# A third scan stage prepared inside the last convolution of a bidirectional RWKV-7 step

## The chip, the core and the metric

The kernel runs on one core of one Trainium2 chip. The metric is the device time of one execution in microseconds (us). The core's engines are PE (TensorE, matrix products; PEld is its weight load), DVE (VectorE), ACT (ScalarE), POOL (GpSimd) and SP (SyncE, which here only issues DMAs). Each engine executes its own instructions in a fixed order, and an instruction that waits holds up the ones behind it on that engine. SBUF is the on-chip memory of 128 partitions, PSUM the small memory in which PE leaves its results.

## The reference, cut to what matters

One layer of a diffusion backbone over 2176 tokens (128 of context, 2048 latent) and 1024 channels: a modulated RMS norm, one input projection, two head groups, one output projection.

```python
h = _rmsnorm(x, norm_g) * (1 + scale) + shift
r, k, v, g_a, b_gate, c_gate, u_conv, g_b = split(h @ w_in)
ya, s_final = _wkv(h, r, k, v, s0)                 # group A: 8 heads of 64, two directions
yb = b_gate * _short_conv(c_gate * u_conv, conv_w) * silu(g_b)      # group B
u = concat([ya * silu(g_a), yb]) @ w_out
out = x + gate * u

# inside _wkv, per token, head and direction:
s_kk = S @ kk_t
S = S * w_t - s_kk (kk_t * a_t)^T + v_t k_t^T
y_t = S @ r_t
```

The state S is a 64 by 64 matrix per head and direction. The kernel does not go token by token: it takes chunks of 64 tokens, for which the recurrence becomes matrix products with the inverse of a triangular matrix.

## The kernel before, in words

**Phase 1** (`phase1`) works on tokens in six blocks, two blocks to a third (`THIRD`). Each third has a recurrence part (`recurrence`: dense products for r, k, v and gate, and the operands of the scan, which go to DRAM as `scr_ops`, 1 MB per stage and direction when read back) and then a convolution part: `groupB` for four channel groups g and the third's two blocks j, eight units in all. Each unit has four dense products (`mmc`, `mmu`, `mmgb`, `mmb`) of 24 matmuls, three per 128 input channels (lines 182 to 184), since each float32 operand is split in a high and a low part. Weight blocks are read by `load_w`: in the first third raw (`raw_w`, tag `wr`, two buffers of 4 KB per partition, in pool `p1w`) and split; the split form is kept in DRAM (`scr_wsp`) and read from there in the later thirds (tag `w`, four buffers). `gate_rows`, run in the second third, uses the `wr` buffers too.

**Phase 2** (`phase2`) is the scan. 17 stages (`stages`), each of 8 chunks per direction gi = 0, 1, go through a software pipeline:

- `L` loads the operands into `rr` (one tile per direction, no second buffer);
- the first products `Gm`, `Fm` (line 1019, 32 small matmuls a direction) and `Qm` (line 1028, 4 transposes a direction) go through PSUM to the slot tiles F, GA and Q by `Ge`, `Fe` (DVE, line 1037), `Fa`, `Qe` (ACT). There are three slots (`B.slots`), and stage s has slot s modulo 3;
- `dg`, `ab` (DVE, line 1063), `zi` (ACT, lines 1072 to 1075), `pre` (DVE, lines 1081 and 1082) prepare, and `I` (`inverse`, POOL, lines 1091 and 1094, 45 instructions) makes the inverses of 32 by 32 blocks in the tile `zt`, of which there are two buffers;
- `zr`, `zd` (DVE, lines 1102 and 1105) transpose it, `U`, `bu`, `W`, `n` (PE line 1119, ACT 1122, PE 1127, ACT 1130; `c0`, `c1` on ACT, line 1111) merge pairs of blocks, `X`, `Xc` (PE 1171, ACT 1175) and `E`, `Ev` (PE 1189, DVE 1194) make the chunk operators, and `gh` copies GA and Q (ACT, lines 1160 and 1161) next to their operands;
- `S`, `sv`, `y` carry the state through the chunks (PE 1220, DVE 1246, ACT 1267).

`SEQ` is one body of the pipeline: `Gm1+3` in body b stands for stage b + 3. Bodies -3 to -1 are a prologue; from body 0 on PE, DVE and ACT have their order written out by hand (`manual_schedule`), and the last bodies follow `LATE`. POOL and SP there, and everything in the convolution and the prologue, are ordered by a planner from its own estimates, earlier lines of the program first.

**The seam between the phases.** In the last third's convolution the generator `early` runs beside the units, four steps after each unit. It opens phase 2's first pools on the right side of SBUF (`setup_first`) and emits the products and inverses of the first stages by `first(s)`, six steps a stage. `main` then opens the rest (`setup_rest`), on the left side where phase 1's pools were, and emits the prologue, which skips what is done already (`done`). A pool's memory can be used again when the tiles that lay there are released; slot 2 was in the pool `p2r2` of `setup_rest`.

Of the kernel before, what the change touches and what calls it, by code (L numbers as in the profile page):

```python
# [62 lines left out]
def phase1(K):  # L63
# [3 lines left out]
    wp = Pool(K, "p1w", "left", 2)  # L67
    hl = Pool(K, "p1h", "left", 2)
    tp = Pool(K, "p1t", "left")
    ca = Pool(K, "p1ca", "right")  # L70
    hr = Pool(K, "p1hr", "right")
    ta_ = Pool(K, "p1ta", "right")
# [68 lines left out]
        return w  # L141

    def raw_w(cb):
        raw = wp.tile([128, 8, 128], F32, tag="wr", name=f"wr{cb}_{K.u()}", bufs=2)
        nc.sync.dma_start(raw[:], A["win"][cb])
        return raw

# [475 lines left out]
    def gate_rows():  # L623
        for b in range(2):
            pr = None
            for k2 in range(4):
                wt = wp.tile([128, 2, 512], F32, tag="wr", name=f"wgate{b}{k2}", bufs=2)
                nc.sync.dma_start(wt[:], A["wada"][4 + b][:, k2 * 2:k2 * 2 + 2])
                yield
                pr = pr or pax.tile([128, 512], F32, tag="ax", name=f"psgr{b}")  # L630
                mod_rows(pr, wt, (k2 * 2, k2 * 2 + 1))
            rows = tp.tile([128, 512], F32, tag="pv", name=f"gaterow{b}", bufs=1)
            P.copy(rows[:], pr[:])
            yield
            pg = pax.tile([2, 512], F32, tag="ax", name=f"psgate{b}")
            T.matmul(pg[:], sel[:], rows[:], start=True, stop=True)
            gr = tp.tile([2, 512], F32, tag="pv", name=f"gate{b}", bufs=1)
            nc.sync.dma_start(gr[:], A["bgate"][:, b * 512:(b + 1) * 512].broadcast_to((2, 512)))
            V.tensor_tensor(gr[:], pg[:], gr[:], ALU.add)
            nc.sync.dma_start(S["gate"][:, b * 512:(b + 1) * 512], gr[:])  # L640
# [32 lines left out]
    for t3, js in enumerate(THIRD):  # L673
        wd, wi = wlora if t3 == 0 else (load_w(32), load_w(33))
        lws = {}
        pre = {}
        for j in js:
            if j not in hs:
                if t3 == 0:
                    pre[0] = psf[2:]  # L680
                    ws = ws0 + [load_w(cb) for cb in (8, 12)]
                    nc.sync.dma_start(smask[:], A["cst"][:, 128:512])
                run(make_h(j, xb[j]))
            lws[j] = lora_down(j, wd, wi, psf[:2] if j == 0 else None)
        if t3 == 0:
            load_up()
        if t3:
            ws = [load_w(cb) for cb in (4, 0, 8, 12)]
        wts = dict(zip("krvg", ws))
        following = {}  # L690
        recurrence(t3, [(g, j) for g in range(4) for j in js], js, lws, pre.pop(0, None), following)
        early = iter(()) if t3 != 1 else (x for f in (first_states, gate_rows) for x in f())
        if t3 == 2:
            for p in (pax, ta_, hr, ca):
                p.close()
            early = K.early()
        for g in range(4):
            ws = [load_w(cb + g) for cb in (20, 24, 28, 16)] if g else [wts[x] for x in "krvg"]
            for j in js:
                groupB(g, j, ws, hs[j], following)  # L700
                following = {}
                for _ in range(4 if t3 == 2 else 2):
                    next(early, None)
            if g == 1 and t3 < 2:
                j, j2 = THIRD[t3 + 1]
                run(make_h(j, norm(j, load_x(j))))
                xb[j2] = norm(j2, load_x(j2))
        for _ in early:
            pass
# [106 lines left out]
def phase2(K):  # L816
# [8 lines left out]
    def setup_first():  # L825

        O.r0 = Pool(K, "p2r0", "right")
        O.rI = Pool(K, "p2rI", "right")
        O.r1 = Pool(K, "p2r1", "right")
        O.pm = Pool(K, "p2m", "right", 2, PSUM)  # L830
        B.msk = O.r0.tile([128, 4, 128], F32, name="msk")
        B.mkg = O.r0.tile([128, 2, 128], F32, name="mkg")
        for i, j in enumerate((0, 2, 4, 5)):
            D(B.msk[:, i], A["msk"][:, j, 0:128])
        for i, j in enumerate((1, 3)):
            D(B.mkg[:, i], A["msk"][:, j, 64:192])
        B.I2 = O.r0.tile([128, 64], F32, name="I2")
        D(B.I2[:], A["i2"])
        B.idt = O.r0.tile([128, 128], F32, name="idt2")
        D(B.idt[:], A["idt"])  # L840
        B.hm = O.r0.tile([128, 2], F32, name="hm")
        D(B.hm[:], A["cst"][:, 514:516])
        B.ph = O.r0.tile([128, 3], F32, name="ph")
        D(B.ph[:], A["cst"][:, 516:519])
        B.slots = []
        for i in range(2):
            new_slot(O.r0)
        B.rr = ring(O.r1, 2, [128, 5, 8, 64], "rr", presetR)

    def new_slot(pool):  # L850
        i = len(B.slots)
# [9 lines left out]
    def setup_rest():  # L861
        O.l0 = Pool(K, "p2l0", "left")
        O.l1 = Pool(K, "p2l1", "left")
        O.pS = Pool(K, "p2S", "left", 4, PSUM)
        O.p2 = Pool(K, "p2s", "left", 2, PSUM)
        O.r2 = Pool(K, "p2r2", "right")
        new_slot(O.r2)
        cp = O.l0
        vec = cp.tile([128, 4], F32, name="vec2")
        D(vec[:], A["vec"][:, V_GW:V_GW + 4])  # L870
        B.gwh = cp.tile([128, 4], F32, name="gwh")
        V.tensor_scalar(B.gwh[:], vec[:], 0.5, None, ALU.mult)
        B.geps = cp.tile([128, 1], F32, name="geps")
        V.memset(B.geps[:], 64e-5)
        B.pc = cp.tile([64, 2, 8, 34], F32, name="pc")
        for d in range(2):
            D(B.pc[:, d], S[f"pc{d}"].rearrange("(e c) n -> c e n", c=64))

        B.fs = ring(O.l1, 2, [128, 2, 2, 8, 64], "stf", presetS)
        B.gs = ring(O.l1, 2, [128, 2, 2, 8, 64], "stg", presetS)  # L880
        B.gs2 = ring(O.r2, 2, [128, 2, 2, 8, 64], "sth", presetS)
        B.zb = O.l1.tile([128, 16, 64], F32, name="zb")
        zero(B.zb)
# [489 lines left out]

    def early():
        setup_first()
        for s in range(2):
            yield from first(s)

    seq = [(w.split("+")[0], int(w.split("+")[1]) if "+" in w else 0) for w in SEQ.split()]
# [6 lines left out]
    def main():  # L1386
# [10 lines left out]
        for word in LATE.split():  # L1397
            n, t = word.split("@")
            if n == "R":
                O.pm.close()  # L1400
                O.r2.close()
                O.r1.close()
                K.last["R"]()
                K.body = NST
            elif n == "Lo":
                for p in (O.p2, O.l1):
                    p.close()
                K.last["Lo"]()
            elif "." in t:
                next(ends[tuple(int(c) for c in t.split("."))], None)  # L1410
            elif n in K.last:
                K.last[n](int(t))
            else:
                do(n, int(t))
# [234 lines left out]
```

## Time and profile before

| | us |
|---|---|
| median of 3 runs | 1580.28 (1579.95 to 1585.35) |
| profiled execution, first to last instruction | 1578.3 |
| its device time around the span | not listed; 2.0 against the median |
| PE busy | 1499.9 (95%) |
| DVE, ACT, POOL busy | 1139.9, 772.3, 573.8 |
| mean granted TensorE clock | 0.982 |

The span is one execution seen by the hardware profiler. Phase 1 takes the first 947 us, the scan's bodies go to about 1340 us with the output projection beginning in between, and the rest is the output projection. In the rows of the profile a number with us is a time from the span's start; psGm, psFm, psQm are the PSUM tiles of Gm, Fm and Qm, `mm...` those of dense products. A busy time of POOL leaves out the short gap between two of its instructions.

### The profile page before, as it was taken

The page shows a single profiled execution, that of the slowest core. Times are in us where ns is not written, and L with a number is a line of the kernel's source. Part 1 is how long each engine was busy: PE and PEld are TensorE (multiplying, and loading weights), DVE is VectorE, ACT ScalarE, POOL GpSimd, SP SyncE. Part 2 cuts the span into 40 slices and gives each one's busy share as a digit, 9 for nine tenths or more (in the row PEclk, how much of TensorE's full clock was granted, in tenths as well). Part 3 has the DMA queues.
Part 4 walks back from the last instruction along what each step waited for, and adds up shares of the span by engine and source line. Part 5 has one row for each costly group of instructions (what it writes and reads, how often), then busy time and mean ns, then how long its engine had stood idle before and what let it go on. Part 6 is the DMA issues. An engine that isn't in the chain of part 4 may idle for free.

```text
span 1578.3 us, 39371 instructions
## 1 busy us (share of the span) xinstructions
PE 1499.9 (95%) x16208; PEld 1381.2 (88%) x16208; DVE 1139.9 (72%) x1957; ACT 772.3 (49%) x1462; POOL 573.8 (36%) x962
## 2 busy tenths in 40 slices
PE   5999999999999999999999998999999998899998
PEld 2899999999999999899998997888888886678786
DVE  5999995764999735449985428798998997746533
ACT  4566652432555213135551107887878777523222
POOL 0133330001333100013322805888788887212221
PEclk7899999999999999999999998999999999999999
DMA  9669998663878865438887537566676754646442
GB/s 371 213 174 264 269 270 332 223 223 115 225 220 217 233 226 180 145 116 233 261 218 267 194 125 178 150 188 159 194 192 179 193 163 149 180 142 188 151 143 93
DMA packets 204579, 313.78 MB, mean 199 GB/s; under 512 B 58088, under 2 KB 147560, under 8 KB 190320
## 3 DMA queue, kind: packets, MB, share of 16 engines
q1 hardware_dynamic: 168816, 311.13, 63.9%
q10 hardware_dynamic: 35584, 0.14, 1.4%
q8 instruction: 127, 2.08, 0.6%
q14 instruction: 52, 0.43, 0.1%
HBM read 208.05 MB, written 103.17 MB: 197 GB/s over the span
## 4 chain that ended last, share of the span: by engine, by line
PE 65%; DVE 14%; POOL 7%; issue 5%; DMA 5%; ACT 2%; SPq 0%; ACTq 0%; DVEq 0%; POOLq 0%
POOL zt L1094 4%; PE psu L1503 4%; PE psu L1504 4%; PE psu L1505 4%; PE psE L1189 3%; POOL ztmp L1091 3%; PE mmb L182 2%; PE mmb L184 2%; PE mmb L183 2%; PE psS L1220 2%; PE mmc L182 2%; PE mmc L184 2%; PE mmc L183 2%; PE mmu L182 2%; PE mmu L184 2%
## 5 line engine op out<-in xcount | busy, mean ns | idle before, releaser
L1094 POOL TENSOR_TENSOR zt<-zt,ztmp 128x30 f32<-128x30 f32 (+7 forms) x510 | 215.4, 422 | 39.8
L1091 POOL TENSOR_TENSOR ztmp<-ab,zt 128x60 f32<-128x60 f32 (+7 forms) x255 | 139.4, 547 | 66.7 <-DVE ab L1082 47.0
L410 POOL TENSOR_TENSOR sh<-rawl 128x384 f32<-128x384 f32 (+1 forms) x48 | 47.5, 1007 | 210.1 <-ACT rawl L401 210.1
L1220 PE MATMUL psS<-sv,E 128*64 128x64 f32 x2176 | 104.6, 229 | 12.8 <-DVE sv L1246 7.3
L1220 PEld LDWEIGHTS psS<-sv,E 128*64 128x64 f32 x2176 | 82.8, 137 | 37.9 <-issue 16.3
L1194 DVE TENSOR_TENSOR E<-psE,msk 128x512 f32<-128x512 f32 x136 | 90.6, 683 | 20.0 <-PE psE L1189 18.9
L1568 POOL TENSOR_TENSOR z<-z,x 128x512 f32<-128x512 f32 x32 | 42.7, 1337 | 147.6 <-DVE z L1562 85.7
L1175 ACT ACTIVATE stf<-psX 64x512 f32<-64x512 f32 x136 | 80.3, 590 | 13.1 <-PE psX L1171 10.7
L434 POOL TENSOR_TENSOR hsl<-sq,hsh 128x384 fp32r<-128x384 f32 (+1 forms) x24 | 34.1, 1421 | 129.9 <-ACT hsh L429 121.6
L1246 DVE TENSOR_TENSOR sv<-psS,pc 64x128 f32<-64x128 f32 x254 | 63.7, 271 | 22.4 <-PE psS L1220 21.7
L182 PE MATMUL mmg<-h,w 128*128 128x384 f32 (+1 forms) x216 | 70.8, 328 | 0.0
L183 PE MATMUL mmg<-h,w 128*128 128x384 f32 (+1 forms) x216 | 70.7, 327 | 0.0
L184 PE MATMUL mmg<-h,w 128*128 128x384 f32 (+1 forms) x216 | 70.7, 327 | 0.0
L219 POOL TENSOR_TENSOR hslq<-ssq,hshq 128x384 fp32r<-128x384 f32 (+1 forms) x4 | 4.8, 1202 | 174.2 <-ACT hshq L218 109.6
L182 PE MATMUL mmb<-h,w 128*128 128x384 f32 (+1 forms) x192 | 63.9, 333 | 4.0 <-DMA w<-scr_wsp 4.0
L182 PE MATMUL mmv<-h,w 128*128 128x384 f32 (+1 forms) x192 | 63.1, 329 | 0.9 <-DVE sg L524 0.6
L184 PE MATMUL mmc<-h,w 128*128 128x384 f32 (+1 forms) x192 | 62.8, 327 | 1.0 <-DVE w L154 1.0
L184 PE MATMUL mmb<-h,w 128*128 128x384 f32 (+1 forms) x192 | 63.7, 332 | 0.0
L183 PE MATMUL mmb<-h,w 128*128 128x384 f32 (+1 forms) x192 | 63.6, 331 | 0.0
L182 PE MATMUL mmu<-h,w 128*128 128x384 f32 (+1 forms) x192 | 63.0, 328 | 0.2
L182 PE MATMUL mmc<-h,w 128*128 128x384 f32 (+1 forms) x192 | 63.0, 328 | 0.0
L184 PE MATMUL mmu<-h,w 128*128 128x384 f32 (+1 forms) x192 | 62.9, 328 | 0.0
(312 smaller groups left out, 5019.6 us busy)
## 6 DMA issues: line engine op xcount, KB each, us to landing
w<-scr_wsp SPq DMA_DIRECT2D x68, 1024.0 KB, 5.4
scr_wsp<-w SPq DMA_DIRECT2D x34, 1024.0 KB, 6.0
rr<-scr_ops SPq DMA_DIRECT2D x32, 1024.0 KB, 6.7
scr_ops<-xs SPq DMA_DIRECT2D x160, 192.0 KB, 6.5
wr<-in_win SPq DMA_DIRECT2D x34, 512.0 KB, 8.2
x<-in_x SPq DMA_DIRECT2D x17, 512.0 KB, 3.9
wadas<-in_wada SPq DMA_DIRECT2D x8, 1024.0 KB, 13.9
sv<-scr_vt SPq DMA_DIRECT2D x32, 256.0 KB, 4.0
```

Source lines behind the costliest of these rows:

```text
L182: T.matmul(ps[:, :n], w[:, 0, k], hh[:, 0, k, :n], start=k == 0, stop=False)
L183: T.matmul(ps[:, :n], w[:, 0, k], hh[:, 1, k, :n], start=False, stop=False)
L184: T.matmul(ps[:, :n], w[:, 1, k], hh[:, 0, k, :n], start=False, stop=k == 7)
L1091: G.tensor_tensor(tv, ab[:, j:j + 2, j + 2:32].unsqueeze(1).broadcast_to((128, kn, 2, n)), zt[:, :kn, j:j + 2].unsqueeze(3).broadcast_to(( ...
L1094: G.tensor_tensor(zt[:, :kn, j + 2:32], zt[:, :kn, j + 2:32], tv[:, :, r], ALU.subtract)
L1175: P.activation(g.fs[64:128, :, hd, e::2], g.ps["X"][e][hr_].rearrange("p a (b t) -> p b a t", b=2), AF.Copy, scale=-1.0)
L1194: V.tensor_tensor(g.E[n][:, k:k + 2].rearrange("p a b c -> p (a b) c"), pe[:].rearrange("p a b c -> p (a b) c"), B.msk[:, ME[g.d]].unsquee ...
L1220: T.matmul(g.sp[i // 4][r, q, hd, :], g.E[n][:, k, hd, r], g.sv[:, u, hd, :], start=True, stop=True)
L1246: V.tensor_tensor(dst, g.sp[i // 4][0:64, q], B.pc[0:64, d, 2 * p:2 * p + 2, c:c + 1].broadcast_to((64, 2, 64)), ALU.mult)
L1503: T.matmul(ps[:], mh[:, n], hi[:, cs], start=start and n == 0, stop=False)
L1504: T.matmul(ps[:], mh[:, n], lo[:, cs], start=False, stop=False)
L1505: T.matmul(ps[:], ml[:, n], hi[:, cs], start=False, stop=stop and n == 3)
```

## The change

The generator `early` runs `first` for three stages, 0, 1 and 2, not for two. For that slot 2 is made in `setup_first`, in a right-side pool of its own, `p2r3`; it is no longer in `p2r2`. To have room for its 20 KB per partition beside the last convolution, the raw weight buffers `wr` move from `p1w` to a pool of their own, `p1r`, the innermost on the left, which is closed before that convolution. In the changed kernel the line numbers of phase 1 grow by one and those of phase 2 behind `setup_rest` by two (the product of line 1019 is in line 1021).

```diff
@@ phase1
     tp = Pool(K, "p1t", "left")
+    wrp = Pool(K, "p1r", "left")
...
     def raw_w(cb):
-        raw = wp.tile([128, 8, 128], F32, tag="wr", name=f"wr{cb}_{K.u()}", bufs=2)
+        raw = wrp.tile([128, 8, 128], F32, tag="wr", name=f"wr{cb}_{K.u()}", bufs=2)
         nc.sync.dma_start(raw[:], A["win"][cb])
         return raw
...
@@ gate_rows
-                wt = wp.tile([128, 2, 512], F32, tag="wr", name=f"wgate{b}{k2}", bufs=2)
+                wt = wrp.tile([128, 2, 512], F32, tag="wr", name=f"wgate{b}{k2}", bufs=2)
...
         if t3 == 2:
-            for p in (pax, ta_, hr, ca):
+            for p in (pax, wrp, ta_, hr, ca):
                 p.close()
             early = K.early()
...
@@ phase2, setup_first
         B.rr = ring(O.r1, 2, [128, 5, 8, 64], "rr", presetR)
+        O.r3 = Pool(K, "p2r3", "right")
+        new_slot(O.r3)
...
@@ setup_rest
         O.r2 = Pool(K, "p2r2", "right")
-        new_slot(O.r2)
...
     def early():
         setup_first()
-        for s in range(2):
+        for s in range(3):
             yield from first(s)
...
             if n == "R":
                 O.pm.close()
                 O.r2.close()
+                O.r3.close()
                 O.r1.close()
```

`first(s)` and `new_slot` are as before:

```python
    def first(s):
        for gi in range(2):
            do(f"L{gi}", s)
        for kinds in (("Gm", "Ge", "dg"), ("Qm", "Qe"), ("Fm", "Fa", "Fe")):
            for gi in range(2):
                for k in kinds:
                    do(f"{k}{gi}", s)
                yield
        for k in ("ab", "zi", "pre", "I"):
            do(k, s)
```

## The prediction

> **What bounds the kernel now.** I read the page's first line, then the busy time in two stretches around the point where the last convolution ends, then the chain through that point, then each engine in order of time.
>
> ```profile
> span 1578.3 us, 39371 instructions
> ```
> ```profile
> 839.20:946.65 107.45, 107.45 (x945) 104.58 (x943) 45.38 (x91) 12.70 (x32) 41.23 (x90) 1.00 0.54 190
> 946.65:970.96 24.31, 18.85 (x459) 16.49 (x459) 18.18 (x36) 21.25 (x40) 8.17 (x20) 0.79 0.84 217
> ```
>
> Columns of the second fence: stretch, length, busy time of PE, PEld, DVE, ACT and POOL with counts, granted clock, DMA share, GB/s. From 839.20 to 946.65 the convolution keeps PE busy without a hole; work added there lengthens it one for one. From 946.65 (last dense product) to 970.96 (first state product S00 of the scan loop) lies a seam in which PE has 5.46 us of idle time and a clock of 0.79. The chain of waits through the seam:
>
> ```profile
> 950.84 0.95 DVE zr L1102
> ...
> 951.85 1.23 PE psU L1119 x64
> ...
> 953.11 0.73 DVE sth L916 x3
> 953.85 0.61 DVE GA L1037
> ...
> 954.50 2.89 PE psFm L1019 x32
> 957.39 1.90 PE psQm L1028 x8
> ...
> 959.54 1.61 PE psW L1127 x61
> 961.15 2.02 PE psFm L1019 x30
> ...
> 967.31 0.75 PE psU L1119 x40
> ...
> 968.53 0.53 PE psU L1119 x21
> 969.06 1.05 PE psGm L1019 x32
> ```
>
> psU, psW, psX, psE are the merge of stages 0 and 1 and the first operators of stage 0, which must come before S00. GA, psFm and psQm up to 961 are stage 2's first products. These are what the change takes away.
>
> Behind the seam the loop is paced by POOL as much as by PE:
>
> ```profile
> 962.34 0.29 POOL L1091 TENSOR_TENSOR ztmp<-ab,zt 128x60 f32<-128x60 f32 x1 [14.51 <-DVE ab L1082]
> ...
> 985.41 1.00 POOL L1094 TENSOR_TENSOR zt<-zt,ztmp 128x30 f32<-128x30 f32 x2
> 986.48 0.29 POOL L1091 TENSOR_TENSOR ztmp<-ab,zt 128x60 f32<-128x60 f32 x1
> ...
> 1332.03 0.31 POOL L1091 TENSOR_TENSOR ztmp<-ab,zt 128x60 f32<-128x60 f32 x1
> ```
> ```profile
> POOL ztmp L1091 <- DVE ab L1082: 17.8, 2, 14.5
> ```
> ```profile
>   POOL zt L1094: 1.1, 3
> ```
>
> Stage 2's inverse runs from 962.34 to 986.41 (24.1 us), stage 3's starts at 986.48, and so on to stage 16's last step at 1332: POOL waits 17.8 us in all, 14.5 before stage 2, so 3.3 in the 370 us after it. The last fence, from the rows of the transpose zr that reads an inverse, says that DVE stood still for POOL for 1.1 us in 17 stages: the two paces are nearly equal.
>
> **The change part by part.** The profiled execution's own device time is not listed; its span is 1578.3, the median of the three runs 1580.3, so 2.0 us lie around the span and the sum is made on 1580.3.
>
> Part 1, stage 2's products enter the convolution. What one stage costs there is read from the two that are there already, lines L1019 (G and F) and L1028 (Q), PE busy second:
>
> ```profile
> 839.20:946.65 107.45, 8.85 (x256) 6.92 (x256) 1.00 0.54 190
> ...
> 839.20:946.65 107.45, 2.36 (x16) 1.91 (x16) 1.00 0.54 190
> ```
>
> (8.85 + 2.36) / 2 = 5.6 us. PE has no idle time there, so **+5.6**. Its evictions, diagonals and transpose lie under PE: with two stages' worth of them in it DVE is busy for 45.38 of 107.45, ACT for 12.70. Without that cover the four G evictions alone would cost 4 times 0.61 (the chain above), 2.4 us. Its two 1 MB loads of rr are issued where they already are, and stage 3's two go ahead, on the queue of the weight loads:
>
> ```profile
> 883.91 0.37 SPq L1009 DMA_DIRECT2D rr<-scr_ops  x1
> 886.44 0.32 SPq L136 DMA_DIRECT2D w<-scr_wsp  x1
> 888.13 0.37 SPq L1009 DMA_DIRECT2D rr<-scr_ops  x1
> ```
>
> Here stage 2's loads already alternate with the weights of group 2, and PE lost nothing; stage 3's will do so with group 3. I take 0 (a rival takes more).
>
> Part 2, the seam without stage 2's products. GA, F, Q, F on the chain are 0.61 + 2.89 + 1.90 + 2.02 = 7.4 us, but something else is late next, on ACT:
>
> ```profile
> 952.63 2.51 ACT L1111 COPY zb<-zd 32x512 f32<-32x512 f32 x4
> 955.17 0.62 ACT L1160 COPY sth<-GA 64x512 f32<-64x512 f32 x1
> ...
> 957.47 1.18 ACT L1122 COPY zd<-psU 32x512 f32<-32x512 f32 x2
> ```
>
> The copies zd<-psU (bu), for which psW waits, end at 958.65; psW started at 959.22. If ACT's order stays, psW moves up by only 0.57. If bu goes ahead of the four sth copies (955.17 to 957.45, 2.28 us), by 2.85. The second has something for it: with slot 2 gone from p2r2, that pool's sth tiles lie (by the pools' order and sizes) on the memory of the convolution's last small tiles, free only after their store, so these copies are ready later. From psW to the operators I take 0.6 (psW and psX run without F between them). PsU of stage 1 and Gm0 of stage 3, from 967.31 to 970.11 = 2.8 us of PE ahead of S00, go into PE's idle time, since rr of stage 3 is there early. Together **-4.0 to -6.3**.
>
> The clock is the third term, by stretch (the clock is the third number from the end):
>
> ```profile
> 950.00:952.00 2.00, 0.15 (x9) 0.15 (x10) 1.97 (x6) 1.48 (x4) 0.00 (x0) 1.00 0.54 137
> ...
> 954.00:956.00 2.00, 1.50 (x20) 1.50 (x24) 2.00 (x4) 1.95 (x4) 0.00 (x0) 0.50 0.93 218
> ...
> 962.00:964.00 2.00, 2.00 (x48) 2.00 (x45) 1.31 (x4) 1.15 (x3) 1.35 (x5) 0.55 1.10 244
> 964.00:966.00 2.00, 1.76 (x56) 1.52 (x48) 0.26 (x1) 1.56 (x3) 1.61 (x6) 1.00 1.08 382
> ```
>
> After the hole ahead of psU (PE busy for 0.15 of the first stretch) PE runs at 0.50 until about 963.5 and is back when stage 2's products have filled it. With these gone PE is emptier for longer: no Gm behind the last dense product, nothing between psU and psW. psX and the first psE may run at 0.50 too. What the low clock costs is bounded by psF, 2.89 us for 32 products at 0.50, and by psX, first in the seam, half of it at the low clock, then in body 0 at the full one:
>
> ```profile
> 963.05 2.35 PE L1171 MATMUL psX<-F,zb 64*64 64x128 f32 x62
> ```
> ```profile
> 986.36 0.87 PE psX L1171 x32
> ...
> 988.46 1.30 PE psX L1171 x32
> ```
>
> 2.35 against 2.17: bounds 0 and, with psX and psE wholly at half rate (0.87 more at most, psX's faster half once again, and as much as that for psE), about +1.5.
>
> The Trainium skill, "TensorE: Matmul & The Clock Gate", Part 1, has the array fall to half rate after an idle window of about 3.4 us and rise after a busy window of the same length. The drop after this hole agrees with it. By that rule alone the moved work, which warmed the clock, would be missed up to S00, and the sum would take the upper bound of +1.5.
>
> Part 3, the inverse of stage 2. Its tile zt has two buffers (L1072); the third is free only when stage 0's zr has been read, and zr writes a tile of the pool p2l1, opened after phase 1 closes:
>
> ```profile
> POOL zb L907 <- PE mmb L184: 40.8, 1, 40.8
> ```
>
> zb of that pool waited for the last dense product. So the inverse will **not** run under the convolution: zr at 950.84, zt's fill, then pre on DVE, now without stage 2's GA, F and transpose ahead of it. zr ends at 951.8 (0.95 in the chain), the fill and pre are three and two short instructions, so an estimate from the gaps of the chain is a start at 954.6 to 956 by the old times; with the convolution's 5.6 at 960.2 to 961.6: 0.7 to 2.1 ahead of 962.34, ending 24.1 later at 984.3 to 985.7. That buys little, because stage 3's inverse also needs its own pre:
>
> ```profile
> 985.25 0.69 DVE L1082 TENSOR_TENSOR ab<-ab,dg 128x512 f32<-128x512 f32 x1
> ```
>
> This ends at 985.94, in the fixed order of body 0, 0.5 us before POOL was free anyway. The start of the POOL train, 986.48, thus moves with body 0 and not with stage 2's inverse, and the 14 inverses behind it keep their pace, (1332.0 - 986.5) / 14 = 24.7 us. I count 0, bounds -0.5 and 0.
>
> Part 4, the pool p1r for raw weights and the pool p2r3 for slot 2: no instruction is added, only addresses change, and there are two raw buffers as before; 0 up to the last convolution. There slot 2 needs no wait, since its memory was the recurrence's.
>
> Sum: +5.6, -4.0 to -6.3, 0 to +1.5, -0.5 to 0: from -1.2 to +3.1. Between these I take +0.7, nearer to the end where bu passes the copies but the clock stays low: 1580.3 + 0.7 = **1581**.
>
> **The rivals.**
>
> *Faster: a whole inverse leaves the loop.* If POOL's lead were kept, 24.1 us of a train that paces the loop would go, against 5.6 in the convolution: 1580.3 - 24.1 + 5.6 = 1562. For it speaks the train without gaps. Against it: zr waits 1.1 us in all, and pre of stage 3 ends only 0.5 us before POOL is free, so that even an inverse finished under the convolution starts the train 0.5 us earlier at most. 5%.
>
> *Slower: stage 3's rr loads come ahead of group 3's weights and PE stands.* Place: the queue from about 910 on. Price: 2 MB at the 382 GB/s of the stretch from 964 to 966 are 5.5 us; the first weights are issued at 910.05, land 5.4 later (median), and PE takes them up where group 2's last product is done, 918.7, 3.2 us of room, so PE would stand 2.3 us. Behind such a hole the clock is halved for about 10 us, as from 954 to 964, which costs dense products half of that, 5 more: 1581 + 7 = 1588.
>
> ```profile
> 910.05 8.96 SPq L136 DMA_DIRECT2D w<-scr_wsp  x4
> ```
> ```profile
> 918.70 0.42 DVE L590 TENSOR_TENSOR bsv<-sg,mmb 128x256 f32<-128x256 f32 x1 [2.04 <-PE mmb L184]
> ```
> ```profile
> w<-scr_wsp SPq DMA_DIRECT2D x68, 1024.0 KB, 5.4
> ```
>
> It decides from a delay of 3.2 us on. Against it: group 2's weights with stage 2's rr lost nothing. 9%.
>
> *The products stay behind the convolution* because the planner puts them there: then the seam is as before and only addresses differ, 1580. PE is full in the convolution, but the two stages before were interleaved without trouble. 6%.
>
> **How the numbers follow.** The forecast has 80%, its own range 1579 to 1584. What a measurement can tell from no change is about 0.5%, 7.9 us: faster means below 1572.4, slower above 1588.2. Faster: the first rival and a little for an order of the seam that I do not see, 0.06. Slower: most of the second, 0.08. Same 0.86. The range takes in the three runs' own spread (1579.95 to 1585.35) and most of the second rival: 1575 to 1587.
>
> **What would show it.** Right: about 16.8 us of L1019 and L1028 in the last convolution and its end at 952; no stage-2 product behind it; the first L1091 of stage 2 behind zr, near 960; stage 3's inverse starting within 2 us of 986.5; POOL without gaps from there. Wrong: an inverse of stage 2 before 950, stage 3's starting before 984, or an idle time of PE above 1 us inside the convolution.

## The result, and the profile after

The changed kernel takes 1593.03 us (median of 5 runs, 1584.24 to 1593.96), the kernel before, run beside it, 1580.49 us. The ratio is 1.0060 with a 95% interval from 1.0039 to 1.0081: 6 to 13 us slower. The forecast was 1581 us, with a range from 1575 to 1587.

The page's first line, and the two stretches of the prediction's first fences again (the convolution, as long a stretch as before; the seam from the last dense product to S00). Columns as there: busy time of PE, PEld, DVE, ACT and POOL, granted clock, DMA share, GB/s.

```profile
span 1591.2 us, 39375 instructions
```
```profile
844.40:951.85 107.45, 105.92 (x1016) 101.43 (x1008) 50.29 (x95) 13.31 (x33) 42.57 (x90) 1.00 0.53 195
951.85:977.50 25.65, 16.16 (x320) 14.59 (x319) 10.50 (x23) 19.98 (x36) 13.16 (x30) 0.60 0.63 125
```

The convolution, full before, now has 107.45 - 105.92 = 1.53 us without PE. The seam has 2.7 us less PE work than before (16.16 against 18.85) and has become longer, 25.65 against 24.31 us; its clock fell from 0.79 to 0.60.

The products of lines L1021 (G and F) and L1030 (Q), first in the convolution, then in the seam; and what PE waited for in the convolution:

```profile
839.20:951.85 112.65, 13.28 (x384) 10.43 (x384) 1.00 0.54 199
951.85:977.50 25.65, 2.22 (x32) 1.80 (x32) 0.60 0.63 125
```
```profile
839.20:951.85 112.65, 3.39 (x24) 2.85 (x24) 1.00 0.54 199
```
```profile
PE psGm L1021 <- DMA rr<-scr_ops: 1.5, 2, 1.1
```

So the third stage's products did move: 13.28 - 8.85 + 3.39 - 2.36 = 5.46 us of PE. The 1.5 us without PE are two waits for loads of rr:

```profile
848.61 1.11 PE L1021 MATMUL psGm<-rr 64*64 64x128 f32 x32 [0.41 <-DMA rr<-scr_ops]
...
895.86 1.11 PE L1021 MATMUL psGm<-rr 64*64 64x128 f32 x32 [1.12 <-DMA rr<-scr_ops]
```

The first stands ahead of stage 0's second Gm, which the change does not touch; the kernel before, profiled a second time (before2 below), waited 1.3 us ahead of stage 0's two Gm. The second stands ahead of stage 2's second Gm and is new.

TensorE in the seam, in order of time:

```profile
958.12 1.92 PE L1121 MATMUL psU<-zr,GA 32*32 32x32 f32 x64 [6.17 <-DVE zr L1104]
962.93 0.23 PE L1129 MATMUL psW<-zb,zd 32*32 32x32 f32 x1 [2.90 <-issue]
...
966.62 5.87 PE L1173 MATMUL psX<-F,zb 64*64 64x128 f32 x64 [0.43 <-ACT zb L1132]
972.43 1.97 PE L1191 MATMUL psE<-stg,stf 128*64 128x128 f32 x16
974.33 1.20 PE L1021 MATMUL psGm<-rr 64*64 64x128 f32 x16
975.46 1.09 PE L1191 MATMUL psE<-stf,stg 128*64 128x128 f32 x14
976.48 1.09 PE L1021 MATMUL psGm<-rr 64*64 64x128 f32 x16
977.50 0.32 PE L1191 MATMUL psE<-stf,stg 128*64 128x128 f32 x1
977.50 0.33 PE L1222 MATMUL psS<-sv,E 128*64 128x64 f32 x2
```

Two holes, 6.17 and 2.90 us, stand where stage 2's products were. Then psX takes 5.87 us; before, its last 62 products took 2.35. Stage 3's Gm still stands ahead of S00. The granted clock:

```profile
954.20:974.60 20.40, 13.16 (x275) 12.20 (x276) 7.08 (x15) 14.99 (x28) 9.70 (x24) 0.50 0.78 151
974.60:992.60 18.00, 16.43 (x369) 14.33 (x371) 14.74 (x27) 9.91 (x20) 9.25 (x22) 1.00 0.39 87
```

It is 0.50 for 20.5 us; before, from 953.6 to 963.8, for 10.2. VectorE and ScalarE have another order:

```profile
952.92 1.41 DVE L918 COPY stf<-I 64x512 f32<-64x512 f32 x4
954.26 1.41 DVE L918 COPY stg<-I 64x512 f32<-64x512 f32 x4
955.60 1.41 DVE L918 COPY sth<-I 64x512 f32<-64x512 f32 x4
956.95 1.03 DVE L1104 STREAM_TRANSPOSE zr<-zt 128x512 f32<-128x512 f32 x1
```
```profile
956.36 0.61 ACT L1162 COPY sth<-GA 64x512 f32<-64x512 f32 x1
...
958.02 0.61 ACT L1163 COPY sth<-Q 64x512 f32<-64x512 f32 x1
958.66 0.63 ACT L1075 ACTIVATE zt<-idt 128x512 f32<-128x512 f32 x1
959.19 2.49 ACT L1113 COPY zb<-zd 32x512 f32<-32x512 f32 x4
...
962.26 1.18 ACT L1124 COPY zd<-psU 32x512 f32<-32x512 f32 x2
```

All presets now stand ahead of zr (before, those of sth stood behind it), and the four copies into sth ahead of the zb copies (before, behind). At the far end, POOL is no longer without a gap:

```profile
992.62 0.28 POOL L1093 TENSOR_TENSOR ztmp<-ab,zt 128x60 f32<-128x60 f32 x1 [7.12 <-DVE ab L1084]
```

Stage 3's inverse starts at 992.62, not 986.48, after POOL stood idle for 7.12 us. Stage 2's inverse starts at 963.1, not under the convolution.

### The profile page after: what moved, and what is told of

The parts are those of the page before. It is cut to its first block, busy times and chain, and to the rows that moved or that the text cites. A ratio compares the mean times of both kernels' runs of the same rounds, so it can differ in the third digit from the quotient of the medians.

```text
span 1591.2 us, 39375 instructions
## 1 busy us (share of the span) xinstructions
PE 1506.4 (95%) x16208; PEld 1387.2 (87%) x16208; DVE 1138.4 (72%) x1957; ACT 771.9 (49%) x1462; POOL 571.9 (36%) x962
## 4 chain that ended last, share of the span: by engine, by line
PE 59%; DVE 14%; POOL 11%; DMA 6%; issue 6%; ACT 2%; SPq 1%; ACTq 1%; DVEq 0%; POOLq 0%
POOL zt L1096 7%; POOL ztmp L1093 4%; PE psu L1506 4%; PE psu L1507 4%; PE psu L1508 4%; PE psE L1191 3%; PE mmb L183 2%; PE mmb L184 2%; PE mmb L185 2%; PE mmc L183 2%; PE mmu L185 2%; PE mmc L185 2%; PE mmu L184 2%; PE mmc L184 2%; PE mmu L183 2%
## 5 line engine op out<-in xcount | busy, mean ns | idle before, releaser
L1096 POOL TENSOR_TENSOR zt<-zt,ztmp 128x30 f32<-128x30 f32 (+7 forms) x510 | 215.1, 422 | 39.8
L1177 ACT ACTIVATE stf<-psX 64x512 f32<-64x512 f32 x136 | 80.3, 591 | 16.0 <-PE psX L1173 13.3
```

The lines of the kernel that those rows point to most:

```text
L1096: G.tensor_tensor(zt[:, :kn, j + 2:32], zt[:, :kn, j + 2:32], tv[:, :, r], ALU.subtract)
L1177: P.activation(g.fs[64:128, :, hd, e::2], g.ps["X"][e][hr_].rearrange("p a (b t) -> p b a t", b=2), AF.Copy, scale=-1.0)
```

## The experiments

All ratios are against the kernel before, run beside the kernel in question. Two lengths are read from every profile: the **convolution**, from the start of stage 0's inverse on POOL to the start of the last dense product, and the **seam**, from there to the start of stage 3's inverse. Before they are 946.53 - 857.9 = 88.6 us and 986.5 - 946.53 = 40.0 us. "Half clock" is how long the granted clock was 0.50 in the seam. The last columns set the two lengths' growth beside the time's, which is (ratio - 1) x 1581.

| kernel | convolution | seam | half clock | growth of the two | growth of the time |
|---|---|---|---|---|---|
| before, second profile | 88.6 | 40.1 | 10.2 | 0.1 | 0.2 |
| the change | 95.7 | 41.0 | 20.5 | 8.0 | 9.5 |
| again | 94.8 | 40.8 | 17.1 | 7.0 | 8.4 |
| range2, range2b | 88.6, 88.7 | 47.1, 43.5 | 20.5, 17.1 | 7.1, 3.6 | 3.8, 4.9 |
| range2o | 88.6 | 47.2 | 27.3 | 7.2 | 2.7 |
| range2q | 88.7 | 40.9 | 13.7 | 1.0 | 0.9 |
| beforeq | 88.7 | 43.0 | 17.1 | 3.1 | 5.2 |
| zt3 | 95.1 | 45.5 | 30.7 | 12.1 | 15.2 |
| warm | 95.4 | 47.5 | 20.5 | 14.3 | 12.8 |
| dense | 95.8 | 46.9 | 10.2 | 14.1 | 13.3 |
| fillu | 95.3 | 46.5 | 23.9 | 13.2 | 10.9 |
| fillb | 88.6 | 41.0 | 6.8 | 1.0 | 2.1 |
| chain2 | 95.3 | 36.8 | 13.7 | 3.5 | 9.8 |
| inconv | 95.9 | 36.3 | 13.7 | 3.7 | 4.3 |
| inconv2 | 96.6 | 39.8 | 23.9 | 7.8 | 6.6 |
| inconv3 | 95.8 | 38.1 | 20.5 | 5.3 | 3.5 |
| gonly | 92.0 | 42.5 | 17.1 | 5.9 | 7.3 |
| gonly2 | 92.3 | 41.7 | 13.7 | 5.4 | 7.1 |

Each row's lengths come from one execution, its time from 4 to 12. That execution can lie far from the median: range2's took 7.5 us more and range2o's 5.4, again's 5.6 less and chain2's 4.6. Over the 19 profiles beside the first the two growths go together (correlation 0.84); chain2 and range2o fall out. What happens ahead of stage 3's inverse is thus most of the story.

### The change once more, and the kernel before once more

**again** is the changed kernel, unedited.

> The changed kernel once more, for a second profile. In the first one the start of stage 3's inverse is 6.1 us later than before (992.6 against 986.5) and the end 12.9 us later (1591.2 against 1578.3), so 6.8 us come after it. If the program makes these 6.8 us, the stretch from that start to the end is 598.6 us again (before: 591.8). If they come from where the granted clock happens to fall in the last 300 us, that stretch changes by some us from run to run and follows the time at half clock, while the seam repeats: stage 3's inverse within 1 us of 992.6.

Measured: 1590.84 us (1583.13 to 1595.27), ratio 1.0053 (1.0026 to 1.0080). The loss is real. The convolution is longer by 7.0 us in the first profile and 6.2 in this one, the seam by 1.0 and 0.9.

**before2** is the kernel before, unedited.

> The kernel before, profiled a second time, with nothing edited. If the 10.2 us at half clock between the last dense product and stage 3's inverse are what its program always gives, they are 8 to 12 us again, the first product of the states (S00) comes 24 to 25 us behind the last dense product and stage 3's inverse 39 to 41 us behind it. If the short stretch was luck of that one execution, the half clock is 17 us or more, S00 comes 26 us or later behind the last dense product, and a gain or loss of 5 us in the seam cannot be read from single profiles.

Measured: 1580.16 us, ratio 1.0001 (0.9978 to 1.0023).

```profile
943.73:967.93 24.20, 18.84 (x458) 16.40 (x458) 18.19 (x36) 21.22 (x40) 8.04 (x20) 0.79 0.83 217
```

Its seam has the length (24.20 against 24.31) and the clock (0.79) of the first profile. The 10.2 us at half clock belong to the program.

### The pools without the third stage

**range2** and **range2b** are one kernel:

```
-        for s in range(3):
+        for s in range(2):
             yield from first(s)
```

> The changed pools alone: raw blocks in p1r, slot 2 in p2r3, but only two stages are prepared in the convolution, so stage 2's products are back behind it. If the moved work makes the loss: the seam is the one of before, psX in it about 2.4 us, stage 3's inverse at 986 to 988, 1580 to 1582. If the new addresses make it (sth tiles on memory of the convolution, slot 2 elsewhere): 1586 or more, with stage 3's inverse at 990 or later.

> The changed kernel with two stages prepared as before, so with the new pools alone, again and with more rounds (the first time it came out at 1586.5 us with an interval from 0.9994 to 1.0054). If the pools move only addresses, its time is that of before, 1580 to 1582 us, ratio 0.998 to 1.002. If the other order that they bring in the seam (all presets ahead of zr, all four sth copies ahead of the zb copies) costs by itself, its time is 1584 to 1588 us, ratio 1.002 to 1.005, and the last dense product to stage 3's inverse takes 42 us or more.

Measured: 1586.47 us, 1.0024 (0.9994 to 1.0054), and with more rounds 1586.72 us, 1.0031 (1.0008 to 1.0054). The second interval leaves out 1: the pools alone cost 1.3 to 8.5 us, though the convolution has its old length. The seam has the order of the changed kernel (VectorE, range2):

```profile
955.83 1.41 DVE L918 COPY sth<-I 64x512 f32<-64x512 f32 x4
957.17 1.04 DVE L1104 STREAM_TRANSPOSE zr<-zt 128x512 f32<-128x512 f32 x1
```

### Order or addresses

**range2o** keeps the new pools and two stages, and brings back the order of VectorE and ScalarE:

```
-        B.gs2 = ring(O.r2, 2, [128, 2, 2, 8, 64], "sth", presetS)
+        B.gs2 = ring(O.r2, 2, [128, 2, 2, 8, 64], "sth")
...
+        with tc.issue_after(B.zlast) if s == 1 else ExitStack():   # copies into sth
...
+        for n in "zr zd c0 c1".split():
+            do(n, 0)
+        with tc.issue_after(B.after):                              # behind stage 0's zd
+            for t_ in B.gs2.tiles:
+                presetS(t_)
```

> The new pools alone, with two stages prepared, and with the seam's order brought back to that of before on VectorE and ScalarE: the presets of sth behind stage 0's zr and zd, the copies into sth behind stage 0's zb copies. If the order is what the pools cost, zr starts 5 us behind the last dense product instead of 6 to 7 with the products of stage 2 still ahead of it, stage 3's inverse comes 38 to 40 us behind it, and the time is that of before, 1580 to 1582 us. If the addresses cost something by themselves, it stays at 1584 to 1588 us with the old order.

**range2q** does the same and puts stage 2's Qm behind U of stage 0 and the first Fm on TensorE, where the kernel before has it:

```
+            if (n, t) in (("Qm0", 2), ("Qm1", 2)):
+                continue
             do(n, t)
+            if (n, t) == ("Fm0", 2):
+                do("Qm1", 2)
+                do("Qm0", 2)
```

> The new pools with two stages prepared, VectorE's and ScalarE's order as in the kernel before, and now TensorE's too: stage 2's Qm behind U of stage 0 and its first Fm instead of ahead of U. If dense products inside the stretch at half clock end it, half clock lasts 10 us again, stage 3's inverse comes 38 to 40 us behind the last dense product, and the time is 1580 to 1583 us. If the pools' addresses or the rest of the order cost it, half clock stays at 17 us or more, stage 3's inverse at 43 us or more, and the time at 1584 to 1588 us.

**beforeq** is the kernel before with stage 2's Qm moved ahead of U of stage 0:

```
+        for n in "L0 L1 Gm0 Gm1 Qm0 Qm1".split():
+            do(n, 2)
...
+                with tc.issue_after(B.qlast) if s == 0 else ExitStack():
                     T.matmul(pu[r1, u, :], ...)
```

> The kernel before with one thing in TensorE's order: stage 2's Qm stands ahead of U of stage 0, as in the kernel with the new pools alone, not behind it. If dense products inside the stretch at half clock end it, half clock is now 17 us or more, psX takes 4.5 to 6 us instead of 2.35, stage 3's inverse comes 42 us or more behind the last dense product, and the time is 1584 to 1588 us. If the place of Qm is nothing, half clock stays at 10 us and the time at 1580 to 1583 us.

Measured: range2o 1583.64 us, 1.0017 (0.9991 to 1.0042); range2q 1583.08 us, 1.0006 (0.9985 to 1.0026); beforeq 1585.83 us, 1.0033 (1.0012 to 1.0053). TensorE in range2q, then in beforeq:

```profile
955.51 1.97 PE L1031 MATMUL psQm<-idt,rr 128*128 128x128 f32 x8
...
962.17 3.41 PE L1175 MATMUL psX<-F,zb 64*64 64x128 f32 x64
```
```profile
950.43 2.90 PE L1019 MATMUL psGm<-rr 64*64 64x128 f32 x32 [6.66 <-DVE GA L1038]
953.26 1.98 PE L1028 MATMUL psQm<-idt,rr 128*128 128x128 f32 x8
```

With the order brought back in these places, the new pools cost nothing that can be measured, and the seam is 40.9 us again. (VectorE's order is not wholly that of before: two evictions of stage 2's Gm still stand ahead of the presets.) With the old addresses and another order, the loss appears. So the pools seem to cost by the order that the planner draws up around them, not by where tiles lie. Three cautions: range2o, with the order of VectorE and ScalarE alone, still had a seam of 47.2 us against the 38 to 40 expected; the intervals of range2b and range2q overlap; and beforeq's edit made more than I meant, for the second half of Gm now waits 6.66 us for an eviction, so it shows that an order of the seam can cost 0.3%, not that Qm's place does. Of my expectation for it, half clock, seam and time came as written; psX at 4.5 us or more did not, since psX had the full clock by then.

### A whole inverse under the convolution

**zt3** gives stage 2's inverse a third zt buffer (paid for with so's):

```
-        st.zt = tl([128, 16, 32], "zt", 2, O.rI)
+        st.zt = tl([128, 16, 32], "zt", 3, O.rI)
...
-            so = tl([64, 2, 64], "so", 7)
+            so = tl([64, 2, 64], "so", 3)
```

> The changed kernel with a third buffer for zt (2 KB, paid with four of the seven buffers for final states), so that stage 2's inverse can run under the convolution. Step 3 of the prediction: stage 2's inverse starts before 930 and ends before 955, but stage 3's still starts with its own pre, and the total is within 2 us of the changed kernel. Rival (POOL's lead is kept and a whole inverse leaves the loop): stage 3's inverse or the ones behind it come 10 us or more earlier, total below 1582.

Measured: 1600.18 us, 1.0096 (1.0058 to 1.0135). POOL, first step of stage 2's inverse, and the seam's clock:

```profile
906.58 0.29 POOL L1093 TENSOR_TENSOR ztmp<-ab,zt 128x60 f32<-128x60 f32 x1
```
```profile
954.40:985.00 30.60, 23.74 (x372) 21.48 (x374) 10.43 (x21) 19.75 (x35) 0.00 (x0) 0.50 0.52 101
```

The inverse moved 56 us ahead, and stage 3's came 5 us later than in the change, after POOL had waited 44.24 us for its pre. An inverse taken off the train buys nothing, since the train starts when stage 3's pre is there. I had expected a total within 2 us of the change; it is 7 to 9 us above. How much of that is the emptier seam (0.50 throughout, PE busy for 23.74 of 30.60 us) and how much the four so buffers that this edit takes away, no run separates.

### Stage 0's chain first

**chain2** is the changed kernel with stage 0's chain ahead of what else stands in the seam:

```
...
+        for n in "gsL0 zr zd U c0 c1 bu gh00 W n".split():
+            do(n, 0)
+        with tc.issue_after(B.after):        # behind stage 0's zd
+            presets()
```

The other copies into stg and sth are put behind stage 0's n (for stage 0) and behind the Xc copies (for stage 1) in the way that range2o shows.

> The changed kernel with one difference in order: on VectorE stage 0's zr and zd stand ahead of the presets of stf, stg and sth, and on ScalarE stage 0's zb copies, bu and n stand ahead of the copies into stg and sth, with one pair of stg copies between them. If the order was what cost the seam its gain, zr starts at 952 to 953 instead of 956.95, psX begins 4 to 6 us sooner behind the last dense product than its 14.8 us, stage 3's inverse 36 to 38 us behind it instead of 40.8, and the time is 1586 to 1589 us. If the clock sets it, TensorE is at half rate until 17 to 20 us behind the last dense product whatever stands first, psX takes 5 us or more again, stage 3's inverse stays 39 to 41 us behind, and the time is 1589 to 1593 us.

Measured: 1591.04 us, 1.0062 (1.0041 to 1.0082). The profiled seam is 36.8 us, as the order theory said; the time is as the clock theory said. Neither explains both. The profiled execution, at 1586.45 us, lies 4.6 us below the median, and why its seam and the median differ stays open.

**inconv** moves zr, zd, U and bu of stage 0 under the convolution, **inconv2** adds an order of ScalarE with the zb copies first, **inconv3** is inconv with bu put into zr's tile. (In the first two, c1 comes after bu and copies U's product, not the inverse's block: values of stage 0 differ, work and waits do not.)

```
+        O.rz = Pool(K, "p2rz", "right")          # zr and zd live here
...
             if (k, s) == ("zi", 2):
+                for n in ("zr", "zd", "U", "bu"):
+                    do(n, 0)
```

> The changed kernel with zr, zd, U and bu of stage 0 moved under the convolution (zr and zd get a place of their own on the right side, which the kernel leaves free there). Stage 2's inverse can then start at 915 to 925, under the convolution too, and in the seam only the zb copies, W and n stand ahead of psX. If the chain of stage 0 sets the seam, psX begins 10 to 11 us behind the last dense product instead of 14.8, stage 3's inverse comes 36 to 38 us behind it, and the time is 1585 to 1589 us. If an emptier seam only means more time at half clock, as the kernel with three zt buffers had it, half clock lasts 25 us or more, stage 3's inverse is no nearer than 41 us, and the time is 1592 to 1600 us.

> As the run with zr, zd, U and bu of stage 0 under the convolution, and with ScalarE's order in the seam changed: the zb copies first, one pair of stg copies, n, and only then the other copies into stg and those into sth. If the chain sets the seam, psX begins 5 to 7 us behind the last dense product, the first psE 11 to 13 us behind it (the stg copies come last), stage 3's inverse 30 to 35 us behind it, and the time is 1578 to 1584 us. If the clock sets it, TensorE runs at half rate from about 3 us behind the last dense product for 20 us or more, stage 3's inverse is 38 us behind or later, and the time is 1588 to 1596 us.

> The first of the two runs with stage 0's zr, zd, U and bu under the convolution, with one thing mended: bu of stage 0 is put into zr's own tile, so that the block that c1 copies into zb stays that of the inverse (in those two runs zb's lower right block of stage 0 held the product instead, which leaves their work and times as they are). If an emptier seam gives back only part of the 5.6 us that the convolution grows, the time is 1583 to 1587 us, ratio 1.001 to 1.004. If the whole way to stage 3's inverse shrinks as far as that of the run before it (36 us behind the last dense product), 1580 to 1583 us. If the first time was chance, 1589 us or more as the changed kernel.

Measured: inconv 1584.74 us, 1.0027 (1.0003 to 1.0052); inconv2 1588.40 us, 1.0042 (1.0018 to 1.0066); inconv3 1587.83 us, 1.0022 (1.0003 to 1.0042). TensorE in inconv3, then in inconv2:

```profile
960.12 0.28 PE L1140 MATMUL psW<-zb,zr 32*32 32x32 f32 x2 [6.48 <-issue]
...
963.62 5.87 PE L1184 MATMUL psX<-F,zb 64*64 64x128 f32 x64 [1.00 <-ACT zb L1143]
```
```profile
961.51 5.87 PE L1184 MATMUL psX<-F,zb 64*64 64x128 f32 x64 [0.68 <-ACT zb L1142]
967.31 0.69 PE L1202 MATMUL psE<-stg,stf 128*64 128x128 f32 x2
969.75 0.48 PE L1202 MATMUL psE<-stg,stf 128*64 128x128 f32 x2 [1.76 <-DMA stf<-scr_ops]
```

These win back part of the loss, and no more (1.0022 to 1.0042 against 1.0053 and 1.0060): psX starts up to 8 us sooner behind the last dense product (6.5 in inconv2, 15.0 in the change), still takes 5.87 us at half clock, and in inconv2 PE then waits 1.76 us for the load of stf.

### Fillers for the clock

All fillers are 128x512 products into a bank that nobody reads (the lines below are those of dense, fillu and fillb; warm takes another bank). **warm** has six behind the last dense product and three behind U of stage 0; **dense** has four more, between n and psE; **fillu** has only three behind U; **fillb** is the kernel before with four in its two holes.

```
+    def warm(n, w, x):
+        for i in range(n):
+            pf = O.pS.tile([128, 512], F32, tag="S", name=f"warm{K.u()}")
+            T.matmul(pf[:], w, x, start=True, stop=True)
...
+            if (n, t) == ("U", 0):
+                warm(3, B.idt[:], zr)
```

> The changed kernel with work for PE in the two holes of the seam: six products of 128 columns by 512 behind the last dense product and three behind psU, results not used, nothing left out. Clock theory (the seam lasts because PE falls to half clock at 954 and stays there to 975): the clock is 1.0 up to psX, psX takes 2.5 us or less, not 5.87, the first psE about 1.1, not 1.97, stage 3's inverse starts 4 to 6 us earlier (987 to 989), 1586 to 1589. Chain theory (the copies on DVE and ACT ahead of psU and psW set the seam): psX gets faster, but the first state product moves by less than 1.5 us and the total stays above 1590.

> The changed kernel with the fillers of the run before (six products of 128x512 behind the last dense product, three behind U of stage 0) and four more: one behind n, one behind each half of psX, and one behind the third psE of stage 0; they compute nothing that is used. If a run of small products alone lets the clock fall, and dense ones between them hold it, TensorE is at half rate for 7 us or less in the seam, psX and psE take 0.3 us per 16 less than half of what they took, and with 3.6 us of fillers on the path the time is 1586 to 1590 us. If fillers can't hold it, half clock is 17 us or more in the seam again and the time is 1594 to 1598 us.

> The changed kernel with three fillers (dense products of 128x512 into a bank that nobody reads) behind U of stage 0, where TensorE stands idle for 2.9 us before psW. If dense products inside the stretch at half clock end it, it lasts 10 to 11 us instead of 17 to 20, psX takes 2.2 to 3.5 us instead of 5.87, stage 3's inverse comes 36 to 38 us behind the last dense product, and the time is 1586 to 1589 us. If they don't, half clock is 17 us or more and the time is 1591 to 1595 us.

> The kernel before with four fillers of 128x512 in the two gaps in which TensorE stands idle in its seam: three near stage 2's first Gm (3.13 us idle), one behind U of stage 0 (1.45 us idle). If dense work keeps or gives back the clock, half clock in the seam is 7 us or less, stage 3's inverse comes 36 to 38 us behind the last dense product instead of 37.9 to 39.8, and the time is 1577 to 1580 us, below that of before. If the fillers only take TensorE's time, half clock is 10 us or more and the time is 1581 to 1585 us.

Measured: warm 1593.92 us, 1.0081 (1.0056 to 1.0106); dense 1595.31 us, 1.0084 (1.0059 to 1.0109); fillu 1591.44 us, 1.0069 (1.0042 to 1.0095); fillb 1583.05 us, 1.0013 (0.9996 to 1.0031). psX in warm; the clock in fillu:

```profile
965.62 3.33 PE L1173 MATMUL psX<-F,zb 64*64 64x128 f32 x41 [0.45 <-ACT zb L1132]
971.63 2.50 PE L1173 MATMUL psX<-F,zb 64*64 64x128 f32 x23 [2.67 <-issue]
```
```profile
954.60:964.70 10.10, 7.34 (x72) 3.74 (x74) 4.02 (x8) 7.91 (x15) 1.89 (x7) 0.50 1.05 211
964.80:971.60 6.80, 5.32 (x187) 4.92 (x187) 1.78 (x2) 3.54 (x6) 5.78 (x14) 1.00 0.68 120
971.70:985.20 13.50, 13.50 (x127) 11.85 (x123) 4.69 (x9) 8.25 (x14) 10.97 (x26) 0.50 0.01 2
```

Fillers move the stretch at half clock (warm: to 967 and later), shorten it (dense: 10.2 us; fillb: 6.8) or split it (fillu), and no version became faster. dense has the least half clock of all three-stage kernels and is the slowest but one: some of its fillers stand between the parts of psX. So more time at full clock did not by itself bring time back.

### Only the G products moved

**gonly** prepares of stage 2 only Gm, Ge, dg and ab in the convolution, with the order of range2q (VectorE's, ScalarE's and the place of Qm); **gonly2** has the order of chain2.

```
-        for kinds in (("Gm", "Ge", "dg"), ("Qm", "Qe"), ("Fm", "Fa", "Fe")):
+        for kinds in (("Gm", "Ge", "dg"), ("Qm", "Qe"), ("Fm", "Fa", "Fe"))[:1 if s == 2 else 3]:
```

> The changed kernel, but of stage 2 only Gm, its eviction, dg and ab are prepared in the convolution (2.2 us of TensorE there instead of 5.5); Qm and Fm stay in the seam, and VectorE and ScalarE have the order of the kernel before (presets of sth behind zr and zd, copies into sth behind the zb copies). If the moved Q and F were what the seam lacked, half clock there is 10 to 14 us, stage 3's inverse 37 to 39 us behind the last dense product, and the time is 1579 to 1583 us. If the order costs whatever is moved, half clock is 17 us or more and the time 1585 to 1590 us.

> As the run with stage 2's G products alone in the convolution, with the order of the earlier run that put stage 0's chain first (zr and zd ahead of all presets, the zb copies, bu and n ahead of most copies). If chain first and cover both help, stage 3's inverse comes 33 to 36 us behind the last dense product and the time is 1576 to 1580 us, below the kernel before. If chain first gives nothing in the time, as it gave the changed kernel nothing, 1581 to 1586 us.

Measured: gonly 1587.31 us, 1.0046 (1.0027 to 1.0066); gonly2 1587.93 us, 1.0045 (1.0024 to 1.0065). Leaving Q and F in the seam as cover does not save the change: the convolution still grows by 3.4 to 3.7 us, the seam by 1.7 to 2.6, and gonly2's time lies above both that I had expected. No version beat the kernel before.

## Why the prediction was wrong

**What bounds the kernel, and Part 3** held. Stage 2's inverse did not run under the convolution, for the reason given, and zt3 showed the other half: even moved there it buys nothing. The first rival (1562 us) is refuted. Only its start was off, 963.1 against 960.2 to 961.6: zr had slid behind the presets and the fill of zt behind the copies into sth (958.66, 7.0 us behind the last dense product; before, 5.3).

**Part 1, +5.6,** was a little too small. From the start of stage 0's inverse to the last dense product, first before, then in the change and in again:

```profile
857.90:946.53 88.63, 88.63 (x754) 86.45 (x753) 33.66 (x71) 9.16 (x23) 41.23 (x90) 1.00 0.45 156
```
```profile
856.01:951.67 95.66, 94.54 (x891) 90.71 (x889) 41.65 (x83) 11.55 (x29) 42.57 (x90) 1.00 0.47 168
```
```profile
854.86:949.71 94.85, 94.52 (x891) 90.70 (x889) 41.76 (x83) 11.54 (x29) 42.64 (x90) 1.00 0.47 169
```

PE is busy for 5.9 us more, 5.5 of them the products as worked out. But "I take 0" for the rr loads was wrong: PE waited for them ahead of stage 2's second Gm, 1.1 us in the change and 0.3 in again. The two make the 7.0 and 6.2 us of the table. The second rival had the right resource at the wrong place (its waiters were to be the first weights of group 3) and too high a price: 0.3 to 1.1 us against the 7 it gave.

**Part 2, -4.0 to -6.3, with the clock at 0 to +1.5,** is where most of the error lies: the seam grew by 0.9 to 1.0 us. Its steps one by one, from the last dense product's start to S00 (together +1.4 us; 0.4 came back from there to stage 3's inverse):

- psW was to come 0.57 to 2.85 us sooner. It came 1.4 sooner (962.93 - 951.67 = 11.3 against 12.7).
- From psW to psX 0.6 was to go. Nothing went (3.7 us against 3.6): psU of stage 1 moved into that place.
- From psX to psE the clock was to cost 1.5 at most. The stretch became 3.0 us longer (5.8 us against 2.8). Part of it is the clock: the psX that I read as half at the low clock had only 16 of its 64 products there. But the clock does not make 5.87 us. In range2q the same 64 products took 3.41 us, nearly all of them at 0.50. So some 0.8 us of the 3.0 fit the clock, and some 2.5 us go with another rhythm within psX: by the start times in the trace, its products start in fours every 0.2 us in range2q, and in the change two to four in that time. In fillu 53 of them took 2.89 us at the full clock, 55 ns each, where the kernel before needed 28:

```profile
967.05 2.89 PE L1173 MATMUL psX<-F,zb 64*64 64x128 f32 x53
```

  A new order of psX's products, drawn up by the planner as that of the seam, would do this. No run changed it alone, so the reason is not shown.
- From psE to S00, 2.8 us of psU and Gm0 were to go into idle time. Only psU went. Gm of stage 3 stands ahead of S00 as before (974.33 and 976.48, 2.29 us), since TensorE's order left it there.

**Part 4, 0,** was the step that I did not work out at all. "Only addresses change" is true of the instructions and false of their order: the planner put all presets ahead of zr and the copies into sth ahead of the zb copies, the reverse of what Part 2 assumed (copies "ready later"). range2b prices it at 1.3 to 8.5 us with nothing else changed, range2q at about none once most of the order is back. In the seam's length it is 3.5 to 7 us, which is as much as the removed products give back: 47.1 and 43.5 us with two stages, 41.0 and 40.8 with three. On that reading a gain of 2.5 to 6.3 us, about that of Part 2, did arrive against range2, and Part 4 took it. Against it stands chain2, whose order was mended in the three-stage kernel without a gain in time. How the loss splits between the two is therefore not settled; that the two together gave nothing back is.

**The sum.** +7.0 in the convolution and +1.0 in the seam are 8.0 us in the first profile, +6.2 and +0.9 are 7.1 in the second, against 9.5 and 8.4 measured. The rest is within what one profile can differ from the median: from stage 3's inverse to the end the changed kernel took 598.6 us in one profile and 593.0 in the other, for the same program, and the kernel before 591.8 and 591.4.

## What to carry to other kernels

A change of pools in a kernel whose order a planner draws up is a change of order: compare every engine's order at the joint, down to the products of one group, before you write 0, or pin it. Work taken from a stretch that is held up by a chain of small steps on other engines buys only what the chain allows, and what was there may have been cover; work put into a stretch that is full costs its full length, loads included. Two landmarks read from each profile (here the last dense product and stage 3's inverse) tell more over many kernels than any single seam.

## What the hardware showed that I had not expected

- At one granted clock the same small products can differ as much as between the two clocks. At 0.50, psX (64x128 products in 64x64 tiles) took 5.87 us in the change and 3.41 in range2q (0.55 on average there); in range2q 32 psF took 2.89 and then 1.98 us, both at 0.50:

```profile
952.69 2.89 PE L1021 MATMUL psFm<-rr 64*64 64x128 f32 x32
...
960.41 1.98 PE L1021 MATMUL psFm<-rr 64*64 64x128 f32 x32
```

  The best of them at 0.50 are slower than at full clock by a factor below 2: psX 53 ns each against 28, psF 62 against 34 (1.10 us for 32), psE 1.97 us for 16 against 1.05.
- A busy TensorE does not get the clock back soon. In range2o it was busy without a hole for 27.2 us at 0.50, all of it 32- to 128-row tiles:

```profile
953.40:980.60 27.20, 27.20 (x400) 24.68 (x396) 13.74 (x24) 19.57 (x37) 16.18 (x37) 0.50 0.66 161
980.70:990.00 9.30, 9.30 (x243) 8.44 (x239) 7.58 (x14) 2.13 (x5) 2.53 (x8) 1.00 0.50 107
```

  By the rule that the prediction cited from the Trainium skill ("TensorE: Matmul & The Clock Gate", Part 1), the fall follows an idle window of about 3.4 us and the rise a busy one. In the change the fall came 2.2 us into the hole of 6.17 us, sooner than that (before, 1.7 us behind a hole of 3.13 us), and range2o's stretch is eight such windows, all of them busy by the profile (which models where a product ends). What went with the rise can be read from the traces. Every half clock of the table is made of whole multiples of 3.41 us, so it can be cut into such windows. Let each product count the columns that it streams, times the share of the 128x128 array that its weights fill: a psX 32, a psE 64, a dense 128x256 product 256. In the 20 profiles, over the whole span, there are 183 windows at half clock in which PE was busy for at least 95%. Where the count was under 1360, the clock stayed down (39 of 39); from 1490 on it was back in the next window (132 of 132); in the 12 between, either. In range2o seven windows counted 380 to 1314, the eighth 1936. At half clock psX alone counts about 1190 a window in the change (64 x 32 in 5.87 us) and 2050 in range2q. So a TensorE busy with a few small tiles at a time stayed at half clock. Why the border lies there, these runs do not show.
- Time at half clock varies from execution to execution of one kernel. Worked out as (1 - mean clock) x 2 x span, it is 52 us on average over 28 runs of the kernel before, 62 and 65 in the changed kernel's two series. Over the runs of one kernel, a microsecond more of it went with about 0.2 us more time (slopes 0.10 to 0.27, in all but the smallest series and fillb, range2q and inconv2), so the 10 to 13 us more would make 2 to 3 us of the loss, if the time follows from the clock and not the other way round.
